# Moving the norm steps of a feature-major decoder layer to other places in the queues of ScalarE, VectorE and TensorE

## Chip, cores and metric

The kernel runs on one core of a Trainium2 chip. The metric is the device time of one execution in microseconds, the median of three runs. A profile of one further execution stands beside it; its times are microseconds from the start of its span, and it says for each instruction when it began, how long it took and what its engine waited for.

## The reference, cut to what matters

One decoder layer on a sequence of 1024 tokens of 1024 features (float32): a gated feed-forward half, two attentions side by side, a second feed-forward half, and a gated embedding.

```python
x = x + 0.5 * swiglu(rms_norm(x, ffn1_norm), ffn1_w_gate, ffn1_w_up, ffn1_w_down)
h = rms_norm(x, mix_norm)
... # both attentions from h @ w_in
x = x + merged @ w_out
x = x + 0.5 * swiglu(rms_norm(x, ffn2_norm), ffn2_w_gate, ffn2_w_up, ffn2_w_down)
x = x + sigmoid(rms_norm(x, ple_norm) @ w_ple_gate) * (p @ w_ple_proj)

def rms_norm(x, g): return x * rsqrt(mean(x * x, -1) + EPS) * g
def swiglu(h, w_gate, w_up, w_down): return (silu(h @ w_gate) * (h @ w_up)) @ w_down
```

So there are four norms over the 1024 features of a token. Each needs the sum of all squares of a token before any scaled value exists, and matrix products wait for the scaled values.

## The kernel before, in words

**Layout.** The residual stream X lies feature-major: 128 features on the partitions, eight chunks of features, tokens along the free axis, in two halves of 512 tokens (called half 0 and half 1, or `a` and `b` in the code). A sum over features is therefore a sum over chunks and then over partitions.

**Precision.** Each operand of a product is split in two: a high part (a cast to fp32r, usually on ScalarE) and a low part (the value minus the high part, on VectorE; for some weights on GpSimd). A product is three matmuls per chunk: high-high, and the two mixed ones. A *block* below is 12 matmuls of 512 columns into one bank: three combinations of four chunks.

**The steps of a norm for one half** (lines 200 to 270). `squares` squares two chunks on ScalarE (L203) and adds them to a running sum: on GpSimd by default (L205). `square` squares one chunk (L212) for the last two chunks, and `fold` adds everything to one 128x512 tile on VectorE (L216, L218). `totals` transposes that tile on TensorE (L222), sums it on ScalarE (L234) or VectorE (L236), adds EPS, and raises it to -1/2 on GpSimd (L245). `repeat` broadcasts the roots along the free axis (L251 on ScalarE, L253 on VectorE), `spread` transposes them back into a bank of PSUM (L222 again). `scaled` multiplies two chunks by gain and root on VectorE (L263), `high` casts them on ScalarE (L267), `low` subtracts on VectorE (L270).

**Where a norm ends and the next product begins.** This happens in four places.

- *First entry* (`first_entry`): the first norm. The squares are taken from a token-major copy of x loaded by SyncE's queue (`load_tokens`, `token_square`), and TensorE meanwhile projects the per-layer embedding (`project`). Then come `plain` products of half 0, then half 1's norm.
- *First down* (`ffn`, the loop over `steps`): the last chunk of the down projection of feed-forward 1. It has seven products i = 0 to 6 of four groups t = 0 to 3; a group (i, t) is one block, and its eviction (L389) adds it to X on VectorE. Half 0 is final after (4, 3), half 1 after (6, 3). `last_norms(i, t, ...)` is called after each group and issues the norm's steps by an order written out by hand. `second_half` goes on with half 1 while TensorE runs the next products on half 0: a table says after which number of issued matmuls `totals`, `repeat`, `spread` and each `scaled`, `high`, `low` are issued. The next products are those of the attention's v and q, k (`nat_steps`, L733).
- *Second entry* (`second_entry`): the same seven products for `w_out` (eviction L387), with `last_norms` called as F["norms"], then the `plain` products of feed-forward 2.
- *Second down*: as first down, for feed-forward 2; the next products are those of the embedding gate (`ple_steps`, L1560). The gate's weights for this are loaded and split at times given by the table that `ple_start` returns: `ple_high` casts the high parts on ScalarE (L136), `ple_low` subtracts the low parts on GpSimd (L146).

**Combinations.** The gate and up products use seven products where eight would be plain. They are called (n, m): n counts the blocks of weights (even: gate, odd: up), m is one of seven. Their right-hand sides B[m] are combinations of half 0 and half 1. `combo_m`, `combo_a` ... `combo_e` make them; a `split` in them is an L112 cast on ScalarE and an L113 subtraction on VectorE. `combo_e` makes B[4], which product (1, 4) is the first to use, and needs the result of `combo_d` (L584, L585). After the entry, the loop over `seqn` runs (1,5), (2,5), (1,6), (2,6), (1,7), (2,7), (1,3), (2,3), (1,4), (2,4) as s = 0 to 9; each step is a product, its eviction (`evict`, L505 to L530), then a combination, then `prep` of the weights four steps ahead (L112, L113). Products (n,6) and (n,7) add up in one bank: (2,7) can't start before (2,6) is evicted by ScalarE (L507). Products (n,5) and (n,3) share another: (n,3) can't start before (n,7)'s eviction has read it on VectorE (L510).

**What sets the order.** Within these places each engine runs its instructions in the order of the program text, and waits with everything behind it when an input isn't ready. Buffers are slots of named tags (GF, RN, PT, Q, ...) that go round in a ring.

Of the kernel before, what the change touches and what calls it, by code (L numbers as in the profile page):

```python
# [18 lines left out]
P = 128  # L19
# [19 lines left out]
def tile_hybrid_decoder_layer(  # L39
# [160 lines left out]
    def squares(N, j, tag, eng=nc.gpsimd):  # L200

        t = slot(tag, [P, 2, 512])
        nc.scalar.activation(t[:], N["x"][:, 2 * j:2 * j + 2, :], AF.Square, scale=D ** -0.5)  # L203
        if "sum" in N:
            eng.tensor_add(N["sum"][:], N["sum"][:], t[:])  # L205
        else:
            N["sum"] = t
# [185 lines left out]
    def ffn(N, wg, wu, wd, next_gain, resid, hid, tags, entry, tail):  # L393
# [201 lines left out]
        def last_norms(i, t, own, tags_=(("PT", "RN", "GF", "RN"), ("GF", "RN", "KH", "KL"), ("PT", "PT", "KH", "KL"))):  # L595
# [3 lines left out]
            if i == 1 and t % 2:  # L599
                squares(a, t // 2, tags_[0][t // 2])  # L600
# [7 lines left out]
            elif i == 5:  # L608
                if t == 0:
                    totals(a, bank("pt"))  # L610
                elif t == 1:
                    squares(b, 2, tags_[1][0])
                    repeat(a)
# [3 lines left out]
                else:  # L617
# [23 lines left out]
        with tc.manual_schedule():  # L641
            entry(dict(m=combo_m, a=combo_a, t=combo_t, l=combo_l, u=combo_u, s=combo_s, load=load, prep=prep, sums=sums, last_sum=last_sum, plain=plain, silu=silu, product=product, evict=evict, norms=last_norms))
            for s, (n, m) in enumerate(seqn):
# [6 lines left out]
                elif s in (2, 4):  # L650
                    combo_e(s // 2 - 1)
# [394 lines left out]
    def mix_start():  # L1046
# [18 lines left out]
        def end(X, N):  # L1065
# [4 lines left out]
            side = second_half(N[1], (24, 66, 16), lambda: bank("pt"), lambda: bank("pt"), ("PT", "PT", "PT", "Q"))  # L1070
            side[40] = [lambda: mx["qk"].update(w=[wsplit(raws["qk"][kh], 4, 256, tags[kh]) for kh in range(2)])]
# [164 lines left out]
    def first_entry(F):  # L1236
# [92 lines left out]
        scaled(N[0], 2, "PT")  # L1329
        project([(5, 0)], ps2)  # L1330
        token_square(1, 0)
# [13 lines left out]
        token_square(1, 3)  # L1345
# [56 lines left out]
    tags = {"raw": {1: ("KH", "KL")}, "sum": {}, "w": ("Q", "Q", "KH", "KL"), "hl": ("WL", "WL", "WL", "WH") + ("PT",) * 6 + ("WL", "WL", "PT")}  # L1402
# [56 lines left out]
    def second_entry(F):  # L1459
# [12 lines left out]
        for i in range(7):  # L1472
# [17 lines left out]
            elif i == 6:  # L1490
                F["load"](0)
            for t in range(4):
# [5 lines left out]
                if (i, t) == (5, 0):  # L1498
                    oproj.prep(0, 6, (0,))
# [124 lines left out]
```

## Time and profile before

| | |
|---|---|
| Median of three runs | 2281.4 us (2280.97 to 2282.05) |
| Profiled execution | 2281.16 us |
| Its span | 2279.4 us |
| TensorE busy | 2231.5 us |
| VectorE busy | 1488.0 us |
| ScalarE busy | 970.9 us |
| GpSimd busy | 833.3 us |
| Mean granted TensorE clock | 0.997 |

The span is what the profiler saw from the first to the last instruction; the profiled execution's own time is 1.8 us longer. In a row of the timeline the first number is the start, the second the time from the start of the first to the end of the last of the merged instructions (x4 says how many), then engine, line, operation, the tile written, the tiles read and the shape; in brackets stands how long the engine had been idle before, and for what. Instructions of one engine overlap by about a tenth of a microsecond at their ends.

### The profile page before, as it was taken

What the parts mean: (1) busy time and instruction counts of PE and PEld (TensorE: products, weight loads), DVE (VectorE), ACT (ScalarE), POOL (GpSimd) and SP (SyncE); (2) the same over time, 40 slices, a digit from 0 to 9 for tenths busy, and PEclk for the clock granted to TensorE, in tenths of its full rate; (3) what the DMA queues carried; (4) which work ended last, traced back from release to release, by engine and by line L of the source; (5) the groups of instructions that cost most, each with busy time, mean ns of one, the idle gap of its engine ahead of it and who ended that gap; (6) DMA issues with size and microseconds to landing.
All of it is one profiled execution on the core that took longest, in us unless ns stands there. A gap on an engine that the chain in (4) does not pass through costs nothing.

```text
span 2279.4 us, 30028 instructions
## 1 busy us (share of the span) xinstructions
PE 2231.5 (98%) x11241; PEld 1888.6 (83%) x11241; DVE 1488.0 (65%) x2179; ACT 970.9 (43%) x1694; POOL 833.3 (37%) x718
## 2 busy tenths in 40 slices
PE   8999999999999999999999999999999999999999
PEld 6788888888879999998988888877888888888777
DVE  6855555597884565656667676888655555778762
ACT  5433333343443555545455563344333333433531
POOL 0144444410024555645466554310544444200221
PEclk9999999999999999999999999999999999999999
DMA  8223232474432222222133246731323232755122
GB/s 314 71 101 125 83 125 83 162 277 148 148 103 91 78 84 70 69 65 72 38 83 103 65 143 199 274 119 59 120 85 124 84 125 83 277 195 193 56 92 94
DMA packets 187522, 278.08 MB, mean 122 GB/s; under 512 B 27752, under 2 KB 109928, under 8 KB 187376
## 3 DMA queue, kind: packets, MB, share of 16 engines
q1 hardware_dynamic: 187376, 276.17, 36.0%
q8 instruction: 88, 1.44, 0.3%
q14 instruction: 58, 0.48, 0.1%
HBM read 192.47 MB, written 75.27 MB: 117 GB/s over the span
## 4 chain that ended last, share of the span: by engine, by line
PE 83%; DVE 9%; issue 3%; DMA 2%; ACT 2%; POOL 1%; SPq 0%; DVEq 0%; ACTq 0%; POOLq 0%
PE ps L487 33%; PE ps L381 15%; PE ps L741 11%; PE ps L733 8%; PE ps L1560 4%; PE ps L1210 4%; PE ps L1005 3%; PE ps L983 3%; DVE H L113 2%; PE ps L932 1%; PE ps L931 1%; DVE RN L907 1%; DVE H L270 1%; ACT H L112 1%; POOL WL L146 0%
## 5 line engine op out<-in xcount | busy, mean ns | idle before, releaser
L381 PE MATMUL ps<-H,H 128*128 128x512 f32 x2184 | 497.9, 389 | 1.9 <-DVE X L389 1.2
L381 PEld LDWEIGHTS ps<-H,H 128*128 128x128 f32 x2184 | 409.2, 188 | 87.7 <-issue 3.1
L487 PE MATMUL ps<-H,WL 128*128 128x512 f32 x1008 | 238.5, 389 | 0.0
L487 PEld LDWEIGHTS ps<-H,WL 128*128 128x128 f32 x1008 | 189.2, 188 | 39.3
L741 PE MATMUL ps<-H,WH 128*128 128x512 f32 x768 | 210.4, 401 | 1.0 <-DVE PT L856 1.0
L741 PEld LDWEIGHTS ps<-H,WH 128*128 128x128 f32 x768 | 136.2, 188 | 23.8 <-DVE PT L856 1.5
L986 DVE TENSOR_TENSOR PT<-ps,PT 128x512 fp32r<-128x512 f32 (+1 forms) x160 | 101.1, 633 | 73.5 <-ACT PT L985 72.8
L146 POOL TENSOR_TENSOR WL<-RAW,WH 128x512 fp32r<-128x512 f32 (+1 forms) x104 | 123.0, 1204 | 67.2 <-ACT WH L136 54.2
L389 DVE SCALAR_TENSOR_TENSOR X<-ps,X 128x512 f32<-128x512 f32 x168 | 108.6, 684 | 48.9 <-PE ps L381 48.9
L487 PE MATMUL ps<-H,Q 128*128 128x512 f32 x576 | 137.4, 389 | 0.0
L733 PE MATMUL ps<-WH,H 128*128 128x256 f32 (+1 forms) x896 | 133.3, 287 | 2.5 <-DVE H L270 1.2
L985 ACT CAST PT<-ps 128x512 fp32r<-128x512 f32 (+1 forms) x160 | 87.5, 548 | 93.7 <-PE ps L983 90.8
L487 PEld LDWEIGHTS ps<-H,Q 128*128 128x128 f32 x576 | 108.1, 188 | 22.5
L733 PEld LDWEIGHTS ps<-WH,H 128*128 128x128 f32 x896 | 117.2, 190 | 4.7 <-DVE H L270 1.7
L487 PE MATMUL ps<-X,WL 128*128 128x512 f32 x480 | 117.2, 393 | 2.8 <-ACT GF L507 2.8
L205 POOL TENSOR_TENSOR PT<-PT,RN 128x1024 f32<-128x1024 f32 x2 | 4.8, 2409 | 296.8 <-ACT RN L203 296.8
L487 PEld LDWEIGHTS ps<-X,WL 128*128 128x128 f32 x480 | 90.9, 190 | 22.6 <-ACT GF L507 3.6
L741 PE MATMUL ps<-H,WL 128*128 128x512 f32 x384 | 108.5, 399 | 0.0
L1005 PE MATMUL ps<-PT,X 128*128 128x256 f32 (+1 forms) x640 | 104.2, 282 | 3.0 <-DVE PT L986 3.0
L944 POOL TENSOR_TENSOR T<-T,l 128x128 f32<-128x128 f32 (+3 forms) x64 | 73.4, 1150 | 90.3 <-DVE l L943 87.8
L1005 PEld LDWEIGHTS ps<-PT,X 128*128 128x128 f32 x640 | 94.2, 190 | 14.5 <-DVE PT L986 5.4
L487 PE MATMUL ps<-H,PT 128*128 128x512 f32 x432 | 103.8, 391 | 1.6 <-ACT PT L112 1.2
(404 smaller groups left out, 4660.8 us busy)
## 6 DMA issues: line engine op xcount, KB each, us to landing
hidden<-PT SPq DMA_DIRECT2D x40, 512.0 KB, 3.1
WH<-in_ffn_w_gate_dram SPq DMA_DIRECT2D x38, 512.0 KB, 5.3
Q<-hidden SPq DMA_DIRECT2D x24, 512.0 KB, 6.4
hidden<-RN SPq DMA_DIRECT2D x22, 512.0 KB, 2.6
RAW<-in_w_in_dram SPq DMA_DIRECT2D x22, 512.0 KB, 4.1
KH<-in_ffn_w_up_dram SPq DMA_DIRECT2D x20, 512.0 KB, 6.1
KL<-in_ffn_w_up_dram SPq DMA_DIRECT2D x20, 512.0 KB, 6.8
T<-in_ffn_w_down_dram SPq DMA_DIRECT2D x20, 512.0 KB, 4.4
```

The source lines that it names most:

```text
L146: ins = eng_lo.tensor_sub(lo[part], raw[part], f(hi[part]))
L381: pe(nc.tensor.matmul(groups[g][t][:], wt[:, b, k, t * P:(t + 1) * P], act[:, a, k, :], start=(fresh and n == 0), stop=(i in (6, 1, 4) and ...
L389: nc.vector.scalar_tensor_tensor(xs, groups[g][t][:], scale, xs, ALU.mult, ALU.add)
L487: pe(nc.tensor.matmul(ps[:], hl[:, a, k, :], rhs(m, b, k), start=(first and i == 0), stop=(final and i == 11), skip_group_check=True))
L733: pe(nc.tensor.matmul(ps[:, :n], hT[t // 4][a][:, k, (t % 4) * P:(t % 4 + 1) * P], w[k // 4][b][:, k % 4, :n], start=(i == 0), stop=(i == ...
L741: pe(nc.tensor.matmul(ps[:], w[a][:, k, :], hT[half][b][:, k, :], start=(i == 0), stop=(i == 23)))
L944: nc.gpsimd.tensor_mul(T[:, :n], T[:, :n], l[:].broadcast_to([P, n]))
L985: high = nc.scalar.copy(pt[:, 0, :width], ps[:, :width])
L986: low = nc.vector.tensor_sub(pt[:, 1, :width], ps[:, :width], f(pt[:, 0, :width]))
L1005: pe(nc.tensor.matmul(o, lh, r, start=(kpair == c and i == 0), stop=(kpair == 0 and i == 3)))
L1210: pe(nc.tensor.matmul(ps[:], w[a][:, k, :], yT[g][b][:, k, half * 512:half * 512 + 512], start=(i == 0), stop=(i == 11)))
L1560: pe(nc.tensor.matmul(ps, pl["w"][d, k // 2][b][:, k % 2, m * P:(m + 1) * P], hT[half][a][:, k, cs], start=(i == 0), stop=(i == 23)))
```

## The change

It moves steps of the norms within the three engines' queues and makes five kinds of edits.

1. *Sums.* The add in `squares` is issued to VectorE by default. GpSimd keeps only those at i = 1. For half 1 the second and third squares are issued without their add, which follows as a step of its own (`more`) behind `low`.
2. *last_norms.* `repeat` of half 0 comes ahead of the squares of half 1 in (5, 1); the four `scaled`, `high` and `low` of half 0 are issued a group earlier each or so.
3. *second_half.* `totals` and `spread` after 32 and 74 matmuls instead of 24 and 66 in first down, after 20 and 40 instead of 14 and 36 in second down. The split of the q, k weights goes from 40 to 48.
4. *Combinations.* `combo_e` is issued at s = 4 and 5 instead of 2 and 4, and the list of tags for weights is longer, since the tag Q is held for that long.
5. *Entries and gate weights.* First entry: the token tiles of half 1 use other tags, so that two loads need not wait for a tag; the squares of half 1 come earlier; `repeat` of half 0 ahead of a split. Second entry: loads and preps of the first weights are issued earlier, and `totals`, `repeat`, `spread` of half 1 come one plain block of TensorE later. Second down: `ple_high` of the last two pieces at (5, 2) instead of i = 6, `ple_low` of both at (5, 3) instead of (6, 1) and (6, 2).

No product, no arithmetic and no tile shape changes. The diff, cut to its core:

```diff
-    def squares(N, j, tag, eng=nc.gpsimd):
+    def squares(N, j, tag, eng=nc.vector):
...
-        if "sum" in N:
+        if "sum" not in N:
+            N["sum"] = t
+        elif eng is None:
+            N["more"] = t
+        else:
             eng.tensor_add(N["sum"][:], N["sum"][:], t[:])
+
+    def more(N):
+        nc.vector.tensor_add(N["sum"][:], N["sum"][:], N.pop("more")[:])
...
             if i == 1 and t % 2:
-                squares(a, t // 2, tags_[0][t // 2])
+                squares(a, t // 2, tags_[0][t // 2], nc.gpsimd)
...
                 elif t == 1:
+                    repeat(a)
                     squares(b, 2, tags_[1][0])
-                    repeat(a)
                 elif t == 2:
                     spread(a, bank("pf"))
                     scaled(a, 0, tags_[2][0])
-                else:
-                    squares(b, 3, tags_[1][1])
                     scaled(a, 1, tags_[2][1])
                     high(a, 0)
-            elif i == 6:
-                if t == 0:
+                else:
+                    squares(b, 3, tags_[1][1], None)
                     scaled(a, 2, tags_[2][2])
                     high(a, 1)
                     low(a, 0)
-                elif t == 1:
+                    more(b)
+            elif i == 6:
+                if t == 0:
                     scaled(a, 3, tags_[2][3])
-                    squares(b, 0, tags_[1][2])
                     high(a, 2)
                     low(a, 1)
+                elif t == 1:
+                    squares(b, 0, tags_[1][2], None)
+                    high(a, 3)
+                    low(a, 2)
+                    more(b)
                 elif t == 2:
                     square(b, 2, tags_[1][3])
-                    high(a, 3)
-                    low(a, 2)
+                    low(a, 3)
                 else:
-                    low(a, 3)
                     square(b, 3)
                     fold(b)
...
-                elif s in (2, 4):
-                    combo_e(s // 2 - 1)
+                elif s in (4, 5):
+                    combo_e(s - 4)
...
-            side = second_half(N[1], (24, 66, 16), lambda: bank("pt"), lambda: bank("pt"), ("PT", "PT", "PT", "Q"))
-            side[40] = [lambda: mx["qk"].update(w=[wsplit(raws["qk"][kh], 4, 256, tags[kh]) for kh in range(2)])]
+            side = second_half(N[1], (32, 74, 16), lambda: bank("pt"), lambda: bank("pt"), ("PT", "PT", "PT", "Q"))
+            side[48] = [lambda: mx["qk"].update(w=[wsplit(raws["qk"][kh], 4, 256, tags[kh]) for kh in range(2)])]
...
-                tok[half, t] = slot((("KH", "KL", "PT", "PT"), ("Q", "Q", "GF", "RN"))[half][t], [P, D])
+                tok[half, t] = slot((("KH", "KL", "PT", "PT"), ("GF", "RN", "Q", "Q"))[half][t], [P, D])
...
+        repeat(N[0], False)
         for k in range(2):
             split_p("w", k, 1, nc.vector)
-        repeat(N[0], False)
...
         scaled(N[0], 2, "PT")
+        token_square(1, 0)
         project([(5, 0)], ps2)
-        token_square(1, 0)
...
         token_square(1, 1)
+        token_square(1, 2)
         project([(5, 1)], ps2)
         low(N[0], 2)
         high(N[0], 3)
+        token_square(1, 3)
         project([(6, 0)], ps2)
-        token_square(1, 2)
...
         project([(6, 1)], ps2)
-        token_square(1, 3)
...
-            elif i == 6:
-                F["load"](0)
...
                     oproj.prep(0, 6, (0,))
+                    F["load"](0)
+                elif (i, t) == (6, 1):
+                    F["prep"](0, 1)
                 elif (i, t) == (6, 2):
-                    F["prep"](0, 1)
-        F["load"](1)
+                    F["prep"](0, 2)
+                    F["load"](1)
         F["plain"](0, 0, (0,))
-        F["prep"](0, 2)
+        F["prep"](0, 5)
+        F["plain"](0, 0, (1,))
         totals(N[1], bank("pf"), False)
-        F["prep"](0, 5)
-        repeat(N[1], False)
-        F["plain"](0, 0, (1,))
-        spread(N[1], bank("av"))
         F["prep"](0, 4)
         F["load"](2)
+        repeat(N[1], False)
+        F["plain"](1, 0, (0,))
+        spread(N[1], bank("av"))
         F["m"](0)
         F["prep"](1, 1)
         F["m"](2)
-        F["plain"](1, 0, (0,))
...
-            side = second_half(N_[1], (14, 36, 7), ps2, ps2, ("PT", "PT", "PT", "Q"))
+            side = second_half(N_[1], (20, 40, 7), ps2, ps2, ("PT", "PT", "PT", "Q"))
...
-        return {3: [lambda X: ple_load(0, (0, 1))], 4: [lambda X: ple_split(0, (0, 1))], 5: [lambda X: ple_load(0, (2, 3))], 6: [lambda X: ple_high(0, (2, 3))],
-                (6, 1): [lambda N: ple_low(0, 2)], (6, 2): [lambda N: ple_low(0, 3)], "end": end}
+        return {3: [lambda X: ple_load(0, (0, 1))], 4: [lambda X: ple_split(0, (0, 1))], 5: [lambda X: ple_load(0, (2, 3))], (5, 2): [lambda N: ple_high(0, (2, 3))],
+                (5, 3): [lambda N: ple_low(0, 2), lambda N: ple_low(0, 3)], "end": end}
```

The list `hl` of both feed-forwards gets five more tags: `"WL", "WL", "WL", "PT", "PT"`.

More of the change, by code (lines that the diff above doesn't have):

```diff
@@ L1400, in products @@
         F["last_sum"](2, nc.vector)
-    tags = {"raw": {1: ("KH", "KL")}, "sum": {}, "w": ("Q", "Q", "KH", "KL"), "hl": ("WL", "WL", "WL", "WH") + ("PT",) * 6 + ("WL", "WL", "PT")}
+    tags = {"raw": {1: ("KH", "KL")}, "sum": {}, "w": ("Q", "Q", "KH", "KL"), "hl": ("WL", "WL", "WL", "WH") + ("PT",) * 6 + ("WL", "WL", "PT", "WL", "WL", "WL", "PT", "PT")}
     X, N = ffn(N, ffn1_w_gate, ffn1_w_up, ffn1_w_down, 1, x, ad[0], tags, first_entry, mix_start())
@@ L1578, in end @@
             weave(seq(*[ple_steps(u) for u in range(8)]), side)
[L1579 to L1580 removed]
+        return {3: [lambda X: ple_load(0, (0, 1))], 4: [lambda X: ple_split(0, (0, 1))], 5: [lambda X: ple_load(0, (2, 3))], (5, 2): [lambda N: ple_high(0, (2, 3))],
+                (5, 3): [lambda N: ple_low(0, 2), lambda N: ple_low(0, 3)], "end": end}
     X, hT = [], []
     tail = ple_start()
[L1584 removed]
+    tags = {"raw": {0: ("RAW", "RAW"), 1: ("WH", "WH"), 2: ("RAW", "RAW"), 3: ("WH", "WH"), 4: ("KH", "KL")}, "sum": {1: "WH", 2: "KL", 3: "KL"}, "w": ("Q", "Q", "KH", "KH"), "hl": ("WL", "WL", "WL", "KL") + ("PT",) * 6 + ("WL", "WL", "PT", "WL", "WL", "WL", "PT", "PT")}
     ffn(N, ffn2_w_gate, ffn2_w_up, ffn2_w_down, 3, xm, ad[1], tags, second_entry, tail)
```

3 lines of the change are left out of this document (removed).

## The prediction

> **What bounds the kernel now.** I read the page first (busy shares), then the waits of TensorE, then the timeline around each of the longest waits.
>
> ```profile
> span 2279.4 us, 30028 instructions
> ...
> PE 2231.5 (98%) x11241; PEld 1888.6 (83%) x11241; DVE 1488.0 (65%) x2179; ACT 970.9 (43%) x1694; POOL 833.3 (37%) x718
> ```
>
> TensorE is the bound, with 48 us of idle time in all. The change alters no product, so it can win only from that idle time and from clock lost to it. Who ended the idle time:
>
> ```profile
> PE ps L222 <- DVE GF L218: 8.2, 3, 5.6
> PE ps L222 <- DVE RN L253: 5.3, 1, 5.3
> PE ps L222 <- ACT PT L251: 4.6, 3, 1.6
> PE ps L222 <- DVE PT L218: 4.4, 3, 2.1
> ...
> PE ps L487 <- ACT GF L507: 2.8, 2, 2.0
> PE ps L487 <- DVE RN L510: 1.6, 2, 0.8
> PE ps L487 <- DVE Y L510: 1.4, 1, 1.4
> ...
> PE ps L733 <- DVE H L270: 1.2, 1, 1.2
> ```
>
> The columns are total, times, longest. The first four are transposes waiting for a fold of half 1 (L218 on GF), for `repeat` in first entry, for `repeat` of half 0 (three times) and for the fold of half 0 (three times); the L487 rows are products around `combo_e`. Together 29.5 us, all at places that the change rearranges. What matters is how much of it a late VectorE lets go.
>
> **Second down, fold of half 0.**
>
> ```profile
> 2149.27 1.06 ACT L203 ACTIVATE GF<-X 128x1024 f32<-128x1024 f32 x1 [1.16 <-DVE X L389]
> ...
> 2152.91 2.40 POOL L205 TENSOR_TENSOR PT<-PT,GF 128x1024 f32<-128x1024 f32 x1
> ...
> 2153.88 0.63 ACT L212 ACTIVATE RN<-X 128x512 f32<-128x512 f32 x1 [2.09 <-DVE X L389]
> ...
> 2156.14 1.49 DVE L218 TENSOR_TENSOR PT<-PT,RN 128x512 f32<-128x512 f32 x2
> ...
> 2157.78 0.63 PE L222 MATMUL ps<-identf,PT 128*128 128x128 f32 x4 [1.95 <-DVE PT L218]
> ```
>
> The square is ready at 2150.3, but its add starts at 2152.9, behind weight splits in GpSimd's queue, and ends at 2155.3; only then the fold. On VectorE the add can follow the square at once. The fold then waits for the last square (2153.88 + 0.63 = 2154.5) alone, its last two adds take 1.5, so the transposes start at about 2156.2: 1.55 gained of the 1.95. The longest of these three waits, 2.1, is first down's, with the same cause: 1.6 there. The third (4.4 - 2.1 - 1.95 = 0.35) is second entry's, where I leave it. Bounds: 0.8 each if the add collides with those splits, 1.95 and 2.1 at most.
>
> **`repeat` of half 0.**
>
> ```profile
> 2163.79 1.06 ACT L203 ACTIVATE GF<-X 128x1024 f32<-128x1024 f32 x1 [2.08 <-DVE X L389]
> ...
> 2164.76 0.60 ACT L251 COPY PT<-rs 128x512 f32<-128x512 f32 x1
> ...
> 2165.41 0.66 PE L222 MATMUL ps<-identf,PT 128*128 128x128 f32 x4 [1.54 <-ACT PT L251]
> 2165.82 13.87 PE L381 MATMUL ps<-H,H 128*128 128x512 f32 x60
> ```
>
> `repeat` stands behind the squares of half 1, which wait 2.08 for an eviction. Ahead of them it runs when that idle time begins, at 2161.7, and TensorE's wait goes whole: 4.6 / 3 = 1.5 in each of the three places (bounds 1.0 and 1.6). What is late next is VectorE, below.
>
> **Second down, fold of half 1.**
>
> ```profile
> 2168.85 0.69 DVE L389 SCALAR_TENSOR_TENSOR X<-ps,X 128x512 f32<-128x512 f32 x1 [1.33 <-PE ps L381]
> 2169.46 1.40 DVE L263 SCALAR_TENSOR_TENSOR PT<-ps,gains,X 128x512 f32<-128x512 f32 x2
> ...
> 2176.55 1.21 DVE L270 TENSOR_TENSOR H<-PT,H 128x1024 fp32r<-128x1024 f32 x1
> ...
> 2179.99 4.49 POOL L146 TENSOR_TENSOR GF<-RAW,T 128x512 fp32r<-128x512 f32 x2
> ...
> 2185.06 3.30 DVE L218 TENSOR_TENSOR GF<-GF,KL 128x512 f32<-128x512 f32 x2
> ...
> 2188.51 1.09 PE L222 MATMUL ps<-identf,GF 128*128 128x128 f32 x4 [5.64 <-DVE GF L218]
> ```
> ```profile
> 2188.00:2190.00 2.00, 1.49 (x6) 1.43 (x7) 0.36 (x1) 0.37 (x3) 0.00 (x0) 0.50 0.14 33
> ```
>
> Two things make this fold late: GpSimd's adds, and `ple_low`'s four subtractions, beside which VectorE's pair of adds takes 3.30 instead of the 1.49 of half 0. The long wait then halves the clock (seventh value after the stretch's length, 0.50). The four transposes take 1.09 instead of the 0.63 at 2157.78; at half the clock for the two microseconds that the row shows and a little beyond, TensorE loses some 1.4, an estimate.
>
> New: from the spread's transposes (start S) VectorE has 0.7 of waiting, four `scaled` pairs (4 x 1.40), five evictions (5 x 0.69), four `low` (4 x 1.21), two adds (2 x 1.21, the `low`'s shape) and the fold (0.69 + 1.49): 19.1. The splits now run early in this stretch, and I add 2.0 for waiting on them: the 3.30 shows 0.9 more for each of two adds, and two or three instructions meet them. So the fold is ready at S + 21.1. TensorE arrives after the transposes, five blocks (0.4 + 13.7) and 20 matmuls at 13.87 / 60 = 0.23 (4.6): S + 18.7. It waits 2.4, partly for the last `high` and `low` of half 0 just before. So of 5.64 + 1.4 I keep 4.5. Bounds: 2.0 (waits like the 3.30 throughout) and 7.0. In all second down gives 1.55 + 1.5 + 4.5 = 7.6.
>
> `ple_high`'s casts come 10 us sooner on ScalarE; they need weights whose load is issued at i = 5, and the cover is the wait for `scaled` ahead of them. I cost it at nothing; should ScalarE wait there 2 us, `high` and the low parts behind it move by as much.
>
> **First down.**
>
> ```profile
> 681.21 2.14 PE L733 MATMUL ps<-WH,H 128*128 128x264 f32 x14
> ```
>
> The same 19.1 on VectorE, with no splits beside it; TensorE arrives after 0.4 + 13.7 + 32 x 2.14 / 14 (4.9) = S + 19.0. A wait of 0.1 to 0.5 replaces the L733 row's 1.2 and the rest of the first row, 8.2 - 5.64 - second entry's 1.84 = 0.7. Net 1.5. First down: 1.6 + 1.5 + 1.5 = 4.6 (bounds 3.0 and 5.5).
>
> **Second entry, up to the products.**
>
> ```profile
> 1536.76 0.63 PE L222 MATMUL ps<-identf,GF 128*128 128x128 f32 x4 [1.84 <-DVE GF L218]
> ...
> 1541.30 0.69 DVE L113 TENSOR_TENSOR KL<-RAW,KL 128x512 fp32r<-128x512 f32 x1 [1.04 <-ACT KL L112]
> ...
> 1556.55 3.02 PE L487 MATMUL ps<-H,PT 128*128 128x512 f32 x12 [0.64 <-ACT PT L112]
> ```
>
> Here VectorE sets the pace until the second product of (2, 2) at 1556.55. `repeat` gives it a start 1.5 earlier; the two adds for half 1 cost 2 x 1.21, of which time that VectorE spent idle between evictions takes up most (1.33 at one of them in second down's row, which has the same order), so I carry 1.5 to the totals. Ahead of half 1's first `scaled` stands a split (1541.30) that waited 1.04 for ScalarE; issued earlier it lies in the wait for GpSimd's power, and its 0.69 goes. So this chain is 2.2 earlier. TensorE has one block less behind the spread and will wait more at the products, which costs nothing as long as VectorE is the later. Bounds 0 and 3.5.
>
> **`combo_e`, in both entries.**
>
> ```profile
> 1583.82 0.68 DVE L113 TENSOR_TENSOR WL<-KL,WL 128x512 fp32r<-128x512 f32 x1
> ...
> 1585.01 1.23 DVE L113 TENSOR_TENSOR X<-Q,X 128x1024 fp32r<-128x1024 f32 x1 [0.51 <-ACT X L112]
> 1585.40 0.58 ACT L507 COPY GF<-ps 128x512 f32<-128x512 f32 x1
> 1586.03 4.61 PE L487 MATMUL ps<-X,WL 128*128 128x512 f32 x12 [1.99 <-ACT GF L507]
> 1586.15 0.68 DVE L113 TENSOR_TENSOR WL<-WH,WL 128x512 fp32r<-128x512 f32 x1
> ...
> 1594.33 3.02 PE L487 MATMUL ps<-T,Q 128*128 128x512 f32 x12 [0.83 <-DVE RN L510]
> ```
> ```profile
> 1588.00:1589.00 1.00, 1.00 (x4) 0.81 (x3) 0.99 (x1) 0.00 (x0) 0.00 (x0) 0.50 0.36 125
> ```
>
> ScalarE's cast for `combo_e` waits for VectorE's `combo_d`, and the eviction that frees (2, 7), at 1585.40, stands behind it. The change takes the cast away from there, so (2, 7) no longer waits. Next late is (1, 3), which waits for VectorE's L510. Ahead of it VectorE loses the subtraction of 1585.01 and the wait for its cast: the next one starts at 1584.4 instead of 1586.15, 1.7 earlier. Ahead of the second L510 a second such wait of about 0.7 goes. So (2, 3) starts 2.4 earlier than 1594.33, after a wait of about 2.1 at (1, 3). First entry has the same queue and lost 0.8 + 1.4 + 0.8 = 3.0 in the L487 rows: 2.4 there too (bounds 1.0 and 3.0). In second entry the bounds are 0.7 and 4.1: the wait of 1.99 was followed by the clock of 0.50, at which one block took 4.61 instead of 13.87 / 5 = 2.8, and the 2.1 that is left may bring these 1.8 again. Other waits as long (1.84, 1.95, 2.1) brought no such loss, so I take none.
>
> The Trainium skill's page "TensorE: Matmul & The Clock Gate", section "Why this matters for your kernels", says to keep gaps between bursts of matmuls under about 3 us for the clock to stay up. The trace disagrees at 1586, where 1.99 was followed by 0.50. By the page the rest of 2.1 costs no clock and the forecast stands; by the row it is 1.8 longer.
>
> **First entry's norm.**
>
> ```profile
> 31.30 0.69 DVE L113 TENSOR_TENSOR WL<-WH,WL 128x512 fp32r<-128x512 f32 x1 [2.02 <-ACT WL L112]
> ...
> 34.85 0.42 DVE L253 COPY RN<-rs 128x512 f32<-128x512 f32 x1
> 35.41 1.08 PE L222 MATMUL ps<-identf,RN 128*128 128x128 f32 x4 [5.34 <-DVE RN L253]
> ```
>
> `repeat` of half 1 stands behind a chain on VectorE that begins with a split, which waited 2.02 for its cast on ScalarE. The change puts one more square (about 1.05 with its read of the sum) ahead of that cast; `repeat` of half 0 ahead of a split gives 0.5 to 0.8 back. So the 5.34 stays, plus 0.2 (bounds: 1.0 lost, 0.6 won). The loads' other order fills a gap in the queue, but nothing at 31.30 waits for a load.
>
> **Sum.** First entry -0.2 + 2.4 = 2.2; first down 4.6; second entry 2.2 + 2.4 = 4.6; second down 7.6: 19.0. From the profiled 2281.16 (span 2279.4 and 1.8 around it): 2262.2. The median shown is 0.2 above the profiled execution, so 2262.3 against 2281.4. All good ends together give 26.7 (2254.5), all bad ones 9.1 without a further loss of clock (2272).
>
> **Rivals.**
>
> *VectorE takes it back.* The gains at the folds are real, but VectorE, which now makes nine adds more, comes out later than my sums, so that entries gain only 1.0 each (the bad end of one, `combo_e` alone of the other), first down 3.3, second down 5: 10.3, 2270.9. For it: in second entry it already sets the pace. Against: it still sits idle in the rows above, 1.33, 1.04 and 2.02.
>
> *Slower: VectorE becomes the bound at all three folds.* Nine adds at 1.21, none hidden, with the waits only renamed: 10.9 more, 2292.1. It decides once VectorE has no idle time between (4, 1) and the products at all. Against it stand the 1.33 idle at 2168.85 and the fold of half 0, whose lateness the rows lay on GpSimd.
>
> *No change.* Time won at a fold is waited for at the next product, so that all four places end when they did: 2281. It would need every place to be held by something the change doesn't touch, such as a load; the waits above name no load.
>
> **How the numbers follow.** The forecast 0.66, the smaller gain 0.24, slower 0.06, no change 0.04. The range leaves out the slow cases and a little on the good side: 2254.5 to 2272. About 0.2% (4.6 us) is what a measurement can tell from no change. Faster 0.90, same 0.04, slower 0.06.
>
> **What would show it.** Right: the L222 waits for L251 gone from TensorE's list; the fold of half 0 in both downs waiting under 0.6; that of half 1 in second down at 1 to 3 with no stretch at clock 0.50; no wait for L507, a new one of about 2 at the first (1, 3) for L510; the 5.3 of first entry still there. Wrong: a wait of half 1's fold above 4 (the splits cost more than 2.0), the products of second entry at the old distance from its totals, or ScalarE waiting for a load at `ple_high`.

## The result and the profile after

The changed kernel took 2258.74 us (median of four runs, 2257.78 to 2258.97), the kernel before on the same chip 2281.58 (2280.97 to 2282.05): a ratio of 0.9899, 95% interval 0.9882 to 0.9916. That is 22.8 us less, where 19.1 were forecast. The profiled execution took 2258.83 us.

From the page of the changed kernel, the span and the busy times:

```profile
span 2257.1 us, 30032 instructions
...
PE 2228.6 (99%) x11241; PEld 1887.7 (84%) x11241; DVE 1490.8 (66%) x2188; ACT 970.6 (43%) x1694; POOL 812.4 (36%) x709
```

TensorE's work is what it was (11241 matmuls), and its idle time has gone from 48 to 28.5 us. The span is 22.3 us shorter, and of these 19.4 are idle time and 2.9 busy time: two stretches at half the clock, behind 1586 and 2188, are gone, and one, behind 1541, is new. By the prediction's estimates of 1.8 and 1.4 for the first two and the 1.9 measured for the third (below), these make 1.3 of the 2.9; where the rest of the busy time went was not followed up. Who ended the idle time that is left (total, times, longest; line numbers are 5 to 7 higher than before: L222 is now L227, L218 L223, L253 L258, L487 L492, L510 L515, L389 L394):

```profile
PE ps L227 <- DVE Q L258: 5.7, 1, 5.7
PE ps L1012 <- DVE PT L993: 2.8, 4, 1.6
PE ps L492 <- DVE Y L515: 2.3, 2, 1.6
PE ps L492 <- ACT PT L112: 2.1, 1, 2.1
PE ps L227 <- DVE GF L223: 1.6, 3, 1.1
...
PE ps L227 <- DVE PT L223: 1.1, 3, 0.5
```

The folds of half 1 (GF) went from 8.2 to 1.6 and those of half 0 (PT) from 4.4 to 1.1. The 4.6 for `repeat` on ScalarE and the 2.8 for the eviction that freed (2, 7) are gone from the list. The 5.3 of first entry is still there (5.7, now on tile Q). The one wait of 2.1 for a cast of weights is new in this size (before: two such waits, 0.6 at most).

The same places in the timeline of the changed kernel, in the order first entry, first down, second entry, second down:

```profile
35.69 1.08 PE L227 MATMUL ps<-identf,Q 128*128 128x128 f32 x4 [5.67 <-DVE Q L258]
...
655.43 0.66 PE L227 MATMUL ps<-identf,PT 128*128 128x128 f32 x4 [0.49 <-DVE PT L223]
...
661.42 0.60 PE L227 MATMUL ps<-identf,PT 128*128 128x128 f32 x4
...
679.71 0.66 PE L227 MATMUL ps<-identf,GF 128*128 128x128 f32 x4 [0.19 <-DVE GF L223]
...
1541.67 7.50 PE L492 MATMUL ps<-H,PT 128*128 128x512 f32 x24 [2.12 <-ACT PT L112]
...
1573.49 2.88 PE L492 MATMUL ps<-X,WL 128*128 128x512 f32 x12
...
1577.93 6.08 PE L492 MATMUL ps<-T,WL 128*128 128x512 f32 x24 [1.56 <-DVE Y L515]
...
2142.88 0.66 PE L227 MATMUL ps<-identf,PT 128*128 128x128 f32 x4 [0.38 <-DVE PT L223]
...
2148.85 0.60 PE L227 MATMUL ps<-identf,PT 128*128 128x128 f32 x4
...
2167.56 1.49 DVE L223 TENSOR_TENSOR GF<-GF,KL 128x512 f32<-128x512 f32 x2
...
2169.11 0.66 PE L227 MATMUL ps<-identf,GF 128*128 128x128 f32 x4 [1.14 <-DVE GF L223]
```

Both kernels issue the same 11241 matmuls, so the k-th matmul of one can be set against the k-th of the other; the difference of their starts says where time was won. Far from the four places it stands still, and it steps at them: 2.5 us ahead after first entry, 8.1 after first down, 7.8 at the end of the attention, 13.3 after second entry, 22.0 at the end. So the steps are 2.5, 5.6, 5.5 and 8.7, with 0.3 lost between.

### The profile page after: what moved, and what is told of

It is laid out like the page before. It is cut to its first block, busy times and chain, and to the rows that moved or that the text cites. A ratio compares the mean times of both kernels' runs of the same rounds, so it can differ in the third digit from the quotient of the medians.

```text
span 2257.1 us, 30032 instructions
## 1 busy us (share of the span) xinstructions
PE 2228.6 (99%) x11241; PEld 1887.7 (84%) x11241; DVE 1490.8 (66%) x2188; ACT 970.6 (43%) x1694; POOL 812.4 (36%) x709
## 4 chain that ended last, share of the span: by engine, by line
PE 87%; DVE 8%; issue 2%; ACT 2%; DMA 1%; SPq 0%; POOL 0%; DVEq 0%; ACTq 0%
PE ps L492 33%; PE ps L386 18%; PE ps L748 11%; PE ps L740 8%; PE ps L1567 4%; PE ps L1217 4%; PE ps L1012 3%; PE ps L990 3%; PE ps L939 1%; PE ps L938 1%; DVE H L113 1%; DVE RN L914 1%; ACT H L112 0%; DMA PT<-in_x_tokens_dram 0%; DVE PT L113 0%
## 5 line engine op out<-in xcount | busy, mean ns | idle before, releaser
L492 PE MATMUL ps<-H,WL 128*128 128x512 f32 x1008 | 238.5, 389 | 0.0
L492 PEld LDWEIGHTS ps<-H,WL 128*128 128x128 f32 x1008 | 189.2, 188 | 39.3
L492 PE MATMUL ps<-H,Q 128*128 128x512 f32 x576 | 137.4, 389 | 0.0
L394 DVE SCALAR_TENSOR_TENSOR X<-ps,X 128x512 f32<-128x512 f32 x168 | 108.3, 682 | 39.1 <-PE ps L386 39.0
L492 PEld LDWEIGHTS ps<-H,Q 128*128 128x128 f32 x576 | 108.1, 188 | 22.4
L492 PE MATMUL ps<-X,WL 128*128 128x512 f32 x480 | 115.3, 389 | 0.0
L492 PE MATMUL ps<-H,PT 128*128 128x512 f32 x432 | 105.3, 395 | 2.3 <-ACT PT L112 2.1
L492 PEld LDWEIGHTS ps<-X,WL 128*128 128x128 f32 x480 | 90.1, 188 | 18.7
```

The source lines that it names most:

```text
L394: nc.vector.scalar_tensor_tensor(xs, groups[g][t][:], scale, xs, ALU.mult, ALU.add)
L492: pe(nc.tensor.matmul(ps[:], hl[:, a, k, :], rhs(m, b, k), start=(first and i == 0), stop=(final and i == 11), skip_group_check=True))
```

## Experiments

Times are medians; the last column is the distance to the changed kernel's 2258.74, and the kernel before had medians of 2281.61 to 2281.78 beside them.

| run | edit | us | ratio to before (95%) | to changed |
|---|---|---|---|---|
| e1_sums_gpsimd | changed, adds back on GpSimd | 2267.13 | 0.9938 (0.9922 to 0.9955) | +8.4 |
| e5_sums_only | before, adds on VectorE at old places | 2278.69 | 0.9985 (0.9975 to 0.9994) | +20.0 |
| e2_combo_old | changed, `combo_e` at its old place | 2263.57 | 0.9920 (0.9905 to 0.9935) | +4.8 |
| e3_repeat_old | changed, `repeat` at its old place | 2264.49 | 0.9923 (0.9908 to 0.9938) | +5.8 |
| e4_ple_old | changed, low parts of the gate at old place | 2258.07 | 0.9896 (0.9881 to 0.9910) | -0.7 |
| e9_no_low_splits | changed, without these low parts | 2257.29 | 0.9893 (0.9878 to 0.9908) | -1.5 |
| e6_side_old | changed, half 1's steps at old numbers | 2263.19 | 0.9918 (0.9903 to 0.9932) | +4.5 |
| e7_entry_early | changed, `repeat` of half 1 earlier still | 2254.08 | 0.9877 (0.9861 to 0.9894) | -4.7 |
| e8_entry_products | e7 and another order of second entry's products | 2253.70 | 0.9877 (0.9862 to 0.9892) | -5.0 |
| e11_sums_w_gpsimd | e8 and three sums of weights on GpSimd | 2252.20 | 0.9870 (0.9855 to 0.9885) | -6.5 |
| e10_side_later | e7 and second down's fold later | 2252.96 | 0.9874 (0.9858 to 0.9891) | -5.8 |
| e12_together | e7, e8, e10 and e11 | 2251.19 | 0.9867 (0.9850 to 0.9883) | -7.6 |

The theory was that of the prediction: each engine's queue held back a step that TensorE waited for, and the gain is the sum of those waits. The rivals were that one part (the engine of the adds) does all of it, and that some parts do nothing. No run puts back second entry's loads, preps and totals, first entry's new order, or the earlier `scaled`, `high` and `low` of half 0; their share is read from the traces alone.

### e1: the adds back on GpSimd

```diff
-    def squares(N, j, tag, eng=nc.vector):
+    def squares(N, j, tag, eng=nc.gpsimd):
...
     def more(N):
-        nc.vector.tensor_add(N["sum"][:], N["sum"][:], N.pop("more")[:])
+        nc.gpsimd.tensor_add(N["sum"][:], N["sum"][:], N.pop("more")[:])
```

> The changed kernel with all running sums on GpSimd again, at their new places. If the engine of the sums makes the folds of half 0 late, both downs' transposes of totals wait about 2 us for the fold again instead of 0.5 and 0.4, second entry stays at 0.3, and the folds of half 1 are later too: 3 to 6 us more than the changed kernel's 2258.7, so 2262 to 2265. If only the places in the queues count, the time stays within 1 us of 2258.7. If VectorE is the tight engine, taking its nine adds (about 1.2 us each) away wins 1 to 3 us.

Measured 2267.13: 8.4 are lost. In the profile 3.2 of them go in first down and 5.4 in second down. The timeline of e1 in second down, GpSimd's queue first, then VectorE's fold and TensorE, and a window behind it (stretch, its length, busy time and count of PE, PEld, DVE, ACT, POOL, then the granted clock, the sixth value behind the length and not the seventh, as the prediction counts):

```profile
2160.05 2.41 POOL L212 TENSOR_TENSOR GF<-GF,RN 128x1024 f32<-128x1024 f32 x1 [10.16 <-ACT RN L203]
...
2162.41 4.53 POOL L146 TENSOR_TENSOR GF<-RAW,T 128x512 fp32r<-128x512 f32 x2
...
2166.90 3.52 POOL L146 TENSOR_TENSOR RN<-RAW,T 128x512 fp32r<-128x512 f32 x2
...
2170.39 2.36 POOL L212 TENSOR_TENSOR GF<-GF,KH 128x1024 f32<-128x1024 f32 x1
2172.77 0.69 DVE L221 TENSOR_TENSOR GF<-GF 128x512 f32<-128x512 f32 x1 [4.15 <-POOL GF L212]
...
2175.20 0.63 PE L227 MATMUL ps<-identf,GF 128*128 128x128 f32 x4 [3.77 <-DVE GF L223]
```
```profile
2176.00:2178.00 2.00, 2.00 (x6) 1.55 (x5) 0.00 (x0) 1.95 (x10) 0.67 (x1) 0.50 0.71 229
```

The second add stands behind 8 us of `ple_low` in GpSimd's queue, VectorE stands idle for 4.15, TensorE for 3.77, and then the clock is halved. This is the queue, told by GpSimd's starts without a gap between 2160 and 2172. The fold of half 0 waits 2.1 again in first down and 1.94 in second down, as before. The expectation was too small because the clock fell twice more than in the changed kernel, at this place and behind first down's fold of half 0. Once the longer waits are taken off (1.6 of the 3.2, and 1.6 + 2.6 of the 5.4), 1.6 and 1.2 are left for that; 8.4 less 2.8 is inside what was expected.

### e5: the adds on VectorE and nothing else

```diff
-    def squares(N, j, tag, eng=nc.gpsimd):
+    def squares(N, j, tag, eng=nc.vector):
...
-                squares(a, t // 2, tags_[0][t // 2])
+                squares(a, t // 2, tags_[0][t // 2], nc.gpsimd)
```

> The kernel before with one part of the change alone: in the downs the running sums' adds at i = 4, 5 and 6 run on VectorE, at their old places in the code; everything else stays. Theory (the engine of the sums is the largest part, since on GpSimd each add waits in a queue behind weight splits): the folds of half 0 in the downs wait 1.5 less each, the fold of half 1 in second down 3 less, second entry 0.5; against it the scaled values and low parts behind an add in VectorE's queue come 1.2 later. 2274 to 2276, against 2281.6 before. Rival (the gain needs the new places as well, since an add in front of scaled holds it back): 2279 or more.

Measured 2278.69, just under the rival's 2279 and well above the theory's 2276: 3.0 gained. The fold waits are gone (half 1's are 0.6 in all), but three others have come, in TensorE's list of waits:

```profile
PE ps L442 <- ACT WL L112: 3.6, 1, 3.6
...
PE ps L733 <- ACT H L267: 2.3, 1, 2.3
PE ps L1560 <- ACT H L267: 2.1, 1, 2.1
```

With the add right behind the square in the text, ScalarE's square and VectorE's add stand ahead of `scaled`, `high` and `low` of half 0, and the next product, on half 0, is late instead. 8.0 of waits pay for those removed, and behind the 3.6 the clock is at 0.50 for 6.8 us, where before it stayed up. So the new engine alone is worth 3.0, the new places without it (e1) 14.5, and both together 22.8, which is 5.3 more than the sum. The three waits above say why: without the new places VectorE's adds hold back other steps. Part of the 5.3 is clock, which fell in e5 and in e1 where it didn't in the changed kernel; how much was not separated.

### e2, e3: `combo_e` and `repeat` back

```diff
-                elif s in (4, 5):
-                    combo_e(s - 4)
+                elif s in (2, 4):
+                    combo_e(s // 2 - 1)
```

> The changed kernel with combo_e at s = 2 and 4 and the shorter list of tags. If ScalarE's eviction behind the cast for combo_e was the cause, both waits for L507 are back and the products from (2,7) to (2,3) take 2.5 us longer in first entry and 3 longer in second: about 2264.3. If VectorE's chain alone sets the pace there, it comes back by under 2 us in all, and 2260.5 at most.

```diff
                 elif t == 1:
-                    repeat(a)
                     squares(b, 2, tags_[1][0])
+                    repeat(a)
```

> The changed kernel with repeat of half 0 behind the squares of half 1 again. If that order made TensorE wait, three waits of about 1.5 us for ScalarE's copy come back: 4.5 to 5 more, 2263.5. If the steps after it are bound by VectorE, the wait comes back, but the later waits at the folds of half 1 shrink by the same time, and the total is up by under 2: 2260.5.

In e2 the short list of tags of before comes back as well. Both lose about what was expected: 4.8 and 5.8, the second 1.0 more. From the lists of TensorE's waits, e2's rows first, then e3's:

```profile
PE ps L492 <- ACT GF L512: 2.2, 2, 1.5
...
PE ps L492 <- DVE RN L515: 1.6, 2, 0.8
```
```profile
PE ps L227 <- ACT PT L256: 4.6, 3, 1.5
```

The very waits of before come back, and the time with them. That e3 loses 1.0 more than expected has its place at (1, 3) of second entry, where no edit was made: the wait there is 1.78 instead of 1.56, and the clock falls behind it. By the starts of the matmuls this costs 1.5; first entry, unedited too, gives 0.6 back.

```profile
1580.37 7.38 PE L492 MATMUL ps<-T,WL 128*128 128x512 f32 x24 [1.78 <-DVE Y L515]
```
```profile
1582.00:1584.00 2.00, 2.00 (x7) 1.54 (x6) 1.37 (x3) 0.59 (x2) 0.00 (x0) 0.50 0.00 0
```

### e4 and e9: the low parts of the last gate

```diff
...
-                (5, 2): [lambda N: ple_high(0, (2, 3))],
-                (5, 3): [lambda N: ple_low(0, 2), lambda N: ple_low(0, 3)], "end": end}
+                6: [lambda X: ple_high(0, (2, 3))],
+                (6, 1): [lambda N: ple_low(0, 2)], (6, 2): [lambda N: ple_low(0, 3)], "end": end}
```

> The changed kernel with ple_high and ple_low of the last two pieces at i = 6, (6,1) and (6,2) again. If GpSimd's subtractions beside the last low parts and the fold of half 1 were the main cause of the 5.6 us wait in second down, a wait of 4 to 6 us is there again, and the clock falls to 0.5 behind it: 3 to 6 more, 2262 to 2265. If the places of the norm's own steps were the cause, the wait stays under 2.5 and the time within 1.5 of 2258.7.

Measured 2258.07: no difference, and the fold's wait is 1.12. So the first theory fell, and the second, that the places of the norm's own steps were the cause, held. GpSimd's rows in e4, then in the changed kernel:

```profile
2154.83 2.69 POOL L146 TENSOR_TENSOR GF<-RAW,T 128x512 fp32r<-128x512 f32 x2 [10.21 <-ACT T L136]
2157.48 4.51 POOL L146 TENSOR_TENSOR RN<-RAW,T 128x512 fp32r<-128x512 f32 x2
```
```profile
2154.37 4.45 POOL L146 TENSOR_TENSOR GF<-RAW,T 128x512 fp32r<-128x512 f32 x2 [8.31 <-DVE KH L268]
2158.78 3.53 POOL L146 TENSOR_TENSOR RN<-RAW,T 128x512 fp32r<-128x512 f32 x2
```

By the spans' clocks the two start within 0.5 us of each other, though the code issues them at other places; counted from TensorE's work, which is 1.5 ahead in e4, those of e4 start 2.0 later. With the adds gone, GpSimd reaches them early by itself: in the changed kernel 9.0 sooner than before, counted from TensorE's work. Before, they stood behind the second add, as GpSimd's rows of the kernel before show (the split of 2179.99 is the prediction's):

```profile
2176.55 3.48 POOL L205 TENSOR_TENSOR GF<-GF,KH 128x1024 f32<-128x1024 f32 x1 [3.40 <-ACT KH L203]
```

That the splits cost something where they now stand is shown by e9.

```diff
     def ple_low(d, q):
         hi = pl["w"][d, q]
-        pl["w"][d, q] = hi, wlow(pl["raw"].pop((d, q)), hi, 2, 512, PLE_W[d][q][1])
+        pl["raw"].pop((d, q))
+        pl["w"][d, q] = hi, hi
```

> The changed kernel without ple_low's four subtractions for pieces 2 and 3 of the gate in second down (left out: the low parts of these two weight pieces; the high parts stand in their place, so the products keep their number). Theory: VectorE's instructions that meet these splits take 1.65 us instead of 1.21, some 2 us in all, so without them the fold of half 1 is ready 1 to 2 earlier, its wait of 1.14 goes and the time falls by about 1.1, to 2257.6. Rival: the fold waits for VectorE's own queue whatever runs beside it: the wait stays and the time too, 2258.7 within 0.7.

Measured 2257.29, 1.5 less; in the profile second down is 1.1 shorter, as expected, and the rest lies ahead of it, where nothing was changed. VectorE's rows in the changed kernel, beside the splits, and in e9, with TensorE's transposes behind them:

```profile
2159.50 1.65 DVE L275 TENSOR_TENSOR H<-PT,H 128x1024 fp32r<-128x1024 f32 x1
...
2161.68 1.72 DVE L275 TENSOR_TENSOR H<-KH,H 128x1024 fp32r<-128x1024 f32 x1
```
```profile
2158.66 1.22 DVE L275 TENSOR_TENSOR H<-PT,H 128x1024 fp32r<-128x1024 f32 x1
...
2160.39 1.22 DVE L275 TENSOR_TENSOR H<-KH,H 128x1024 fp32r<-128x1024 f32 x1
```
```profile
2167.41 0.66 PE L227 MATMUL ps<-identf,GF 128*128 128x128 f32 x4 [0.38 <-DVE GF L223]
```

### e6 and e10: when TensorE arrives at the fold

```diff
-            side = second_half(N[1], (32, 74, 16), ...)
-            side[48] = ...
+            side = second_half(N[1], (24, 66, 16), ...)
+            side[40] = ...
...
-            side = second_half(N_[1], (20, 40, 7), ps2, ps2, ("PT", "PT", "PT", "Q"))
+            side = second_half(N_[1], (14, 36, 7), ps2, ps2, ("PT", "PT", "PT", "Q"))
```

> The changed kernel with the points at which half 1's scaled values and high and low parts are put into the products after the folds back at their old numbers: 24 and 66 with the splits at 40 in first down's tail, 14 and 36 in second down's. Theory: the fold's transposes stand at the first of these points, so TensorE arrives 8 products of 0.14 us and 6 of 0.23 us sooner and waits that much longer for a fold whose time VectorE sets: +1.1 and +1.4, 2261.2 against 2258.7. Rival: the side list's later part moves sooner as well and gives the time back, 2258.7 within 1.

Measured 2263.19: 4.5 lost, nearly twice what the theory said, of which the profile shows 0.5 in first entry, where nothing was changed. Second down in e6, the transposes and the clock behind them:

```profile
2170.76 0.66 PE L227 MATMUL ps<-identf,GF 128*128 128x128 f32 x4 [2.84 <-DVE GF L223]
```
```profile
2172.00:2174.00 2.00, 2.00 (x6) 1.52 (x6) 0.00 (x0) 1.95 (x7) 1.01 (x1) 0.50 0.73 253
```

The wait grew by 1.7, near the 1.4 expected; what wasn't expected is that the clock is halved behind 2.84 of idle time, and not behind the changed kernel's 1.14. First down lost 1.0, as expected, and second down 2.9.

The other way, from e7 as the base:

```diff
-            side = second_half(N_[1], (20, 40, 7), ps2, ps2, ("PT", "PT", "PT", "Q"))
+            side = second_half(N_[1], (26, 46, 7), ps2, ps2, ("PT", "PT", "PT", "Q"))
```

> The run with the early repeat in first entry, and second down's tail takes the fold's transposes behind 26 products instead of 20 and the scaled values from the 46th instead of the 40th. Theory (the order's numbers only say when TensorE arrives at a fold that VectorE finishes at its own time): six products of 0.23 us cover the wait of 1.14, which goes: 2254.1 - 1.1 = 2253.0. Rival: what follows from the fold comes later by as much as TensorE waits less, and the products of half 1 wait instead: 2254.1 within 0.5.

Measured 2252.96 (2251.95 to 2255.32), 1.1 under e7. Its runs spread over 3.4 us and those of e7 over 1.4, so the medians alone would not show it; the profile shows it at the place itself: second down is 1.4 shorter and the wait is gone.

```profile
2165.55 0.60 PE L227 MATMUL ps<-identf,GF 128*128 128x128 f32 x4
```

### e7, e8, e11, e12: what is left in the entries

```diff
         F["prep"](0, 1)
+        repeat(N[1], False)
...
-        repeat(N[1], False)
...
-        spread(N[1], bank("av"))
+        spread(N[1], bank("pf"))
```

> The changed kernel with repeat of half 1 in second entry moved ahead, right behind prep of piece (0, 1), with the spread into another bank that is free by then. Theory: in second entry VectorE's and ScalarE's chain from the spread sets when the products can start, so an earlier spread is an earlier end: 2.5 to 3 less, about 2256.0. Rival: the fold of half 1 is what the spread waits for, or the wait moves to the next product: 2258.7 within 1.

The expectation names second entry; the edit, and the wait of 5.67 that it is aimed at, stand in first entry. Measured 2254.08, 4.7 less where 2.5 to 3 were expected. The transposes start 2.9 sooner than in the changed kernel, and the step in the profile is 3.6, since the clock is at 0.50 for 3.4 us there instead of 6.8:

```profile
32.77 0.63 PE L227 MATMUL ps<-identf,Q 128*128 128x128 f32 x4 [2.71 <-DVE Q L258]
```

`repeat` no longer stands behind a low part, two evictions and a split on VectorE. What holds it now is a split on VectorE that waits 2.72 for its cast on ScalarE.

```diff
         ps = F["product"](1, 1)
         F["prep"](2, 1)
+        if early:
+            F["prep"](2, 2)
+            F["a"](1)
...
-        F["a"](1)
-        products(F)
+        products(F, True)
```

> As the run with the early repeat, and in second entry prep of (2, 1) and (2, 2) stand ahead of the second half's a(1), whose cast on ScalarE waits 2.20 us for VectorE and keeps prep's cast behind it. Theory: product (2, 1) no longer waits 2.12 and the clock does not halve behind it (24 products in 7.50 us instead of about 5.6 to 6.1): another 1.5 to 3, about 2254. Rival: VectorE's low parts for the products set the time, and the wait only changes its name: as the run with the early repeat, within 1.

Measured 2253.70 (2251.86 to 2255.76): no difference from e7, the rival was right. Where it went, in e8: the product of 1541 starts 3.7 sooner against e7, without the wait and at full clock. Of this 1.2 go at the next plain product, which waits for VectorE's L517, and 2.0 some 35 us later, where (1, 3) waits and the clock falls:

```profile
1570.59 7.34 PE L492 MATMUL ps<-T,WL 128*128 128x512 f32 x24 [2.09 <-DVE Y L515]
```
```profile
1537.00:1539.00 2.00, 2.00 (x10) 1.65 (x10) 2.00 (x3) 0.00 (x0) 0.00 (x0) 1.00 0.00 0
...
1572.00:1574.00 2.00, 2.00 (x6) 1.52 (x6) 1.59 (x3) 0.37 (x1) 0.00 (x0) 0.50 0.00 0
```

In the first window VectorE (third pair) is busy all 2.00. So 0.5 is left of the 3.7. In second entry VectorE is the later of the two: a wait taken from TensorE there came back at the next places where VectorE was needed, and the halved clock with it. So the next run takes work from VectorE.

```diff
-        F["sums"](1, nc.vector)
+        F["sums"](1, nc.gpsimd if early else nc.vector)
```

> The run with the products of second entry in the other order, and there the three sums of weight piece 1 (3 x 0.69 us on VectorE, which is busy without a gap from 1533 to 1570) are formed on GpSimd, which is idle in this stretch. Theory: VectorE sets the pace of second entry's products, so 2 us off its queue are 2 us less wait for L515 at (1, 3): about 2251.7. Rival: the wait comes from the loop between ScalarE's casts, VectorE and the evictions, or GpSimd's longer instructions hold piece (1, 5) and VectorE's beside them: 2253.7 within 1, or above.

Measured 2252.20 (2251.40 to 2252.84), 1.5 under e8 where 2.0 were expected; e8's runs spread over more than that, so it is again the profile that places it. The wait at (1, 3) fell from 2.09 to 0.51 and the clock stayed up, which gives 3.0 at that place. But 1.4 was lost ahead of it: the sums need nothing but their weights, so GpSimd ran them sooner than VectorE had, beside `repeat`. GpSimd's and VectorE's rows in e11, then VectorE's in the changed kernel:

```profile
1524.55 1.26 POOL L460 TENSOR_TENSOR WH<-WH 128x512 f32<-128x512 f32 x1
1524.61 1.49 DVE L258 COPY GF<-rs 128x512 f32<-128x512 f32 x1 [0.90 <-POOL rs L250]
```
```profile
1529.93 0.43 DVE L258 COPY GF<-rs 128x512 f32<-128x512 f32 x1 [0.91 <-POOL rs L250]
```

> The three edits to the changed kernel together: the early repeat in first entry, second entry's products in the other order with the sums of piece 1 on GpSimd, and second down's fold behind 26 products. They act at three separate places, so by the theory they add up: 2252.2 - 1.1 = 2251.1. Rival: the fold's 1.1 is given back behind it, 2252.2.

Measured 2251.19 (2250.95 to 2251.28): the three add up, and this version is 7.6 under the changed kernel. In the profile second down is 1.4 shorter than in e11, so the fold's gain holds; first entry is 1.1 longer, since there the clock fell in e12 and not in e11.

## Why the prediction was right, point by point

Faster was forecast and came, 3.6 under the forecast time and in the range. By the sites, forecast against the steps of the k-th matmul: first entry 2.2 and 2.5, first down 4.6 and 5.6, second entry 4.6 and 5.5, second down 7.6 and 8.7. The range was added up unevenly: its ends take second down's fold of half 0 and `repeat` at their middle. With their own bounds the ends are 27.3 and 7.8, or 2253.9 and 2273.4; the measured time lies inside either way.

**Fold of half 0.** Right: 1.55 in second down, where the wait of 1.95 is now 0.38, and as much in first down. The reason held too: with the engine alone changed back (e1) the waits are 1.94 and 2.1 again.

**`repeat` of half 0.** Right, three times 1.7 for 1.5. The 0.2 is overlap: in a run of matmuls one takes 0.39 and the next starts 0.23 behind its start, so a wait that goes whole gives its idle time and these 0.16. In second down the starts were 1.93 apart before and 0.23 after. Undone, the step costs 5.8 (e3): three times 1.7, and the rest by the clock behind (1, 3).

**Fold of half 1 in second down.** Two terms were mis-sized and one reason was wrong. VectorE was to be ready at S + 21.1; with S = 2148.85 it was at 2167.56 + 1.49 = 2169.05, S + 20.2. TensorE was to arrive at S + 18.7, and did at 2169.11 - 1.14 = S + 19.1. So a wait of 1.14 was left instead of 2.4, and 5.4 were gained instead of 4.5. Of the 2.0 set for collisions with the splits, e9 bears out 1.1. Of the "two things" that made this fold late, GpSimd's adds did, as e1 and its queue show, and the splits beside it cost time too (e9). The reason that was wrong is why they now run early: the new place of `ple_low` in the code does nothing (e4), because the splits come forward by themselves once the adds are gone. `ple_high` at nothing was right by the same run.

**First down.** Its fold of half 1 waits 0.19, as forecast (0.1 to 0.5), and the L733 wait of 1.2 is gone; that place gave some 2.4 instead of 1.5. The waits of before, 1.22 (684.57) and 0.73, less 0.19 make 1.8 of it:

```profile
686.79 0.63 PE L222 MATMUL ps<-identf,GF 128*128 128x128 f32 x4 [0.73 <-DVE GF L218]
```

The rest is the overlap again, 0.16 at each of the two, and some 0.3 at a short stall of the matmuls at 682.8 that is gone.

**Second entry up to the products.** 2.6 for 2.2, but not as smoothly as forecast. TensorE was 12.6 ahead in front of (2, 1) and 10.4 behind it: it waits 2.12 there, and the clock is halved behind it, so that 24 matmuls take 7.50 instead of 5.60. The prediction's "will wait more at the products, which costs nothing" had the wait and left out these 1.9 of clock. That VectorE is the later of the two there, which I carried, is what e8 and e11 show; this is why taking wait and clock loss away in e8 won only 0.5.

**`combo_e`.** Right in kind: no wait for ScalarE's eviction is left, and a wait at (1, 3) for L515 has come, 1.56 for the 2.1 forecast in second entry and 0.78 in first. The gain is 2.5 and 2.9 for 2.4 and 2.4, with the clock at (1, 3) full, as taken:

```profile
1578.00:1580.00 2.00, 2.00 (x9) 1.66 (x10) 2.00 (x3) 0.00 (x0) 0.00 (x0) 1.00 0.08 28
```

That the clock stayed up was luck in part. At this same place it fell behind waits of 1.78 (e3), 2.00 (e10) and 2.09 (e8), and not behind 1.73 (e1) and 1.75 (e6); a wait of the 2.1 that was forecast could well have cost the 1.8.

**First entry's norm.** Right: the wait is 5.67 for 5.34, and the transposes start 0.3 later; behind them TensorE is hardly later than before (under 0.1).

**The rivals.** "VectorE takes it back" didn't happen in the change, but e5 shows where it does: with the adds at the old places, 8.0 of new waits. The slower rival and the rival of no change are excluded by the measured time: the slowest of the four runs is 22 under the fastest before.

## What to carry to other kernels

An engine for a step is chosen together with its place in that engine's queue: here the engine alone gave 3.0, the places alone 14.5, both 22.8. A wait of TensorE is worth its length only as long as the engine that ends it isn't also the one that ends the next wait; where VectorE is busy without a gap, first take work from it. And count what the clock may add to a wait: here from 1.78 on.

## What the runs showed of the hardware

**The clock and short idle times.** Behind idle times of TensorE of 1.2 to 1.6 us the clock stayed up in all these runs. Behind 2.84 (e6), 3.77 (e1) and the 5.64 of second down before, it fell to 0.50 for 3.4 us; behind 3.59 (e5) and the 5.3 to 5.7 of first entry for 6.8. Between, it went both ways: 1.78 at (1, 3) was followed by half the clock in e3, 1.84 and 1.95 in the kernel before were not; before first down's transposes 2.07 was in e1, and 2.08 (659.45, before) was not. The same 2.71 in first entry went both ways; the windows behind it, in e7 and then in e8:

```profile
33.00:35.00 2.00, 2.00 (x9) 1.62 (x8) 2.00 (x4) 0.09 (x1) 0.00 (x0) 0.58 1.02 388
```
```profile
33.00:35.00 2.00, 2.00 (x12) 1.70 (x11) 2.00 (x4) 0.05 (x1) 0.00 (x0) 1.00 1.03 392
```

So the length of the wait alone doesn't decide. It may be why the times of e8 and e10 spread over 3.9 and 3.4 us, where those of most others lie within 1.5; that was not tried. The Trainium skill's page "TensorE: Matmul & The Clock Gate", Part 1 on the clock gate, says that the window over which the hardware judges activity runs free, so that the same kernel meets it at other phases; the two windows agree with that. Its figure, some 3.4 us idle before the clock drops, does not agree: here 1.78 was enough.

**GpSimd beside VectorE.** A subtraction of two SBUF tiles of 128x1024 on VectorE took 1.22 alone and 1.65 to 1.72 beside `ple_low`; `repeat`'s copy took 0.43 alone and 1.49 beside a GpSimd subtraction of 1.26; the 1.06 more are nearly the whole of that subtraction. The Trainium skill's page "SBUF — State Buffer", section "Who interferes with whom", says that VectorE and GpSimd share a pair of ports, that a VectorE instruction with two SBUF inputs contends there with what GpSimd reads from SBUF, and that a copy in a mode which uses both ports and a GpSimd instruction keep each other out for a whole instruction. The rows agree: the subtractions are 0.4 to 0.5 longer, the copy by nearly a whole instruction. That the copy ran in such a mode is not shown by a row.
